# An FFN by seven-product units: 350 tokens become 700 and 348, summed in three PSUM banks, with partial outputs in DRAM

## The chip, the cores and the metric

The kernel runs on one core of one Trainium2 chip. The metric is the device time of one execution in microseconds (us), and the median of several executions is compared. The engines of the core run side by side, each with its own queue of instructions: TensorE (PE for matmuls, PEld for weight loads), VectorE (DVE), ScalarE (ACT), GpSimd (POOL) and SyncE (SP), which here only issues DMAs.

## The reference

One inference step of a two-layer trunk: an SSD (Mamba-2) mixer, a feed-forward network (FFN), an RG-LRU mixer, and a second FFN, with RMS norms before and after each. 1048 tokens go through it: 8 sample tokens, 16 meta tokens and 1024 prompt tokens. The change is in the FFN alone, which runs twice, once in each layer:

```python
D_MODEL = 1024
D_FF = 4 * D_MODEL

def sq_relu_mlp(x, w1, w2):
    h = jax.nn.relu(x @ w1)
    return (h * h) @ w2

# in the trunk, for layer i
h = rms_norm(x, p["norm_ffn_pre"][i])
x = x + rms_norm(sq_relu_mlp(h, p["ffn_w1"][i], p["ffn_w2"][i]), p["norm_ffn_post"][i])
```

All inputs and outputs are float32.

## The kernel before

**Numbers.** Features lie on the 128 partitions and tokens along the rows. Every float32 matrix is split into two float16 parts, hi and lo, and a product of two 128-row tiles takes three matmuls (hi by hi, hi by lo, lo by hi) that add up in PSUM. The tokens are cut into chunks of 350, 350 and 348 (`CW`, `WC`).

**Weights.** They come from DRAM in strips of 1 MB (1024 rows by 256 columns) on SP's queue, into a buffer `ws` of which there are two. A lane of work (`wlane`, `wconv`) turns strip after strip into float16 parts: DVE finds a bound, POOL spreads it over the partitions (`wgb`), a few DVE instructions of one column make the scale, ACT writes hi and DVE lo (`split`) into a buffer `wh`, of which there are five. `self.ahead` limits how many buffers may be ready ahead of their use; a strip of the kinds `H` and `S` (below) takes two, `wh` and `wp`.

**Order of work.** The code writes the matrix products in order and calls `tick()` between them; a tick lets every other lane (weights, norms, sums) emit one step. The engine queues are filled from this by a planner that knows instruction costs, but each engine then works strictly through its own queue.

**The FFN.** The hidden units are taken in four blocks `b` of 1024. For each block the first product gives the hidden units (four strips of `w1`), which are squared and stored as parts in `H`; the second product (four strips of `w2`) adds its part of the output to `acc`, a float32 buffer in SBUF. In the first product of block 0 (`first_phase`, then strip 3) and in the second product of block 3 (`last_phase`, which also runs the norms) every product is done in full, three matmuls for each tile of the sum (`bundle`). The others use Winograd's form of Strassen's algorithm: a strip gives two tiles of 128 outputs, the contraction is taken as pairs of tiles, the chunk as two halves of tokens, and seven products of quarters (`product`) replace eight. For this the sums of the quarters of the weights (`sums`, made by POOL in the strip's own buffer), of the input (`input_sums`, into `TT`) and of the hidden units (`t_sums`, into `HT`) are needed as float16 parts. `t_sums` is a chain over three engines: four POOL subtractions, then ACT writes hi and DVE lo. In the second product only the first `NSUM = 2` of four pairs go by the seven products; the others are added as plain quadrants (`quadrant`).

**A unit** (`unit`) is one strip by one chunk: seven products with 175 (174) moving columns, in seven half banks of four PSUM banks (`pa` to `pd`); eight banks are handed out in turn (`mm`). One ACT copy and five or six DVE instructions add the products up into `z`, which takes one of four buffers (`RBUF`). For the first product `z` then goes through Relu, the squares and `t_sums`; for the second it is added to `acc`.

Of the kernel before, what the change touches and what calls it, by code (L numbers as in the profile page):

```python
# [10 lines left out]
F32 = mybir.dt.float32  # L11
# [12 lines left out]
KT = 8  # L24
# [12 lines left out]
NSUM = 2  # L37
RBUF = 4
# [39 lines left out]
class Queue:  # L78
    """An engine; while hold is set its instructions are issued in program order, and later ones behind them."""
# [38 lines left out]
class Body:  # L118
# [18 lines left out]
    def tab(self, *args, **kw):  # L137
        """An activation whose function needs a table set: these stay in program order."""
# [13 lines left out]
    # ---------------------------------------------------------------- setup  # L152
    def setup(self):
# [28 lines left out]
        # pre-norm gains and group-norm gains scaled by a power of two so that hi/lo fit float16  # L182
# [13 lines left out]
        # the inputs of the ffn leave room for sums of four  # L196
# [15 lines left out]
        self.mad = [self.dram.tile([P, KT * w], F32, name=f"mad{c}") for c, w in enumerate(WC)]  # L212
        a = self.a
# [22 lines left out]
        self.nhid = 0  # L236
        self.wl = self.wlane()
# [7 lines left out]
    def pow2(self, b, n, pool, tag):  # L245
        """p = the power of two at or below b; s = 2^14 / p."""
# [9 lines left out]
    # -------------------------------------------------------------- weights  # L256
# [14 lines left out]
    def split(self, w, st, s, parts):  # L271
        """w = float16 hi and lo parts of st * s, s [P, parts] by contiguous column ranges."""
# [67 lines left out]
    def quarter(self, s, inv):  # L340
        """Scales that leave room for sums of four."""
# [31 lines left out]
    def product(self, ps, i, w, B, T, npair):  # L373
        """ps = one of the seven products of quarters over the first pairs of k tiles, three passes of the float16
        parts; open for the products of the other pairs where there are any."""
# [5 lines left out]
        if npair < 4:  # L381
            add = {2: (0, 0), 3: (0, 1), 4: (1, 0)}.get(i)
        else:
            add = None
        ops = [(lq(l, k), rq(r, k)) for k in range(npair) for l, r in ((0, 0), (0, 1), (1, 0))]
        if add:
            ops += self.quadrant(w, B, npair, *add)
        self.chain(ps, ops)
# [63 lines left out]
    def bundle(self, ps, w, m, act, c, kts=range(KT), first=True, last=True):  # L452
        """ps += sum over k of w[k, m tile]^T act[k, chunk c], three passes of the float16 parts."""
# [14 lines left out]
    def new_u(self):  # L468
        """Float16 parts of the normed input by chunk and k tile."""
# [28 lines left out]
    def normed(self, x, ss, i, hi, lo, pool):  # L498
        """Steps: the pre-norm i of a chunk (its k tiles in x), as float16 parts in hi and lo [P, KT, n]."""
# [1159 lines left out]
```

## Time and profile before

| | |
|---|---|
| runs | 2831.25, 2833.0, 2836.62 us; median 2833.0 us |
| profiled execution | span 2836.7 us from the first to the last instruction; no time of that execution around its span is given, and the span is 3.7 us over the median of the runs |
| instructions | 56933, of them 23209 matmuls |
| PE, DVE, ACT, POOL busy | 2583.1, 2110.1, 1322.6, 691.4 us |
| granted TensorE clock | 0.968 of full speed in the mean |
| FFN of layer 0 | first product of block 0 from about 1004 us; its second product 1095 to 1212; blocks 1 to 3 up to 1668; last product and norms to about 1757 |
| FFN of layer 1 | 2077 to 2167, 2167 to 2737, 2737 to the end |

A line of the profile's groups names the engine, the operation, what it writes and reads (`z<-z,mm`: into `z` from `z` and the PSUM tile `mm`), the shape, the count, the busy time and the mean of one. Nearly all lines of the code appear as line 89, a helper that records every operation, so that instructions are told apart by their tiles and shapes. A table of stages gives, for a stretch of time, what each engine was busy and how many instructions it ran. A table of waits gives who waited for whom: total us, times, and the longest one.

### The profile page before, as it was taken

What the parts mean: (1) busy time and instruction counts of PE and PEld (TensorE: products, weight loads), DVE (VectorE), ACT (ScalarE), POOL (GpSimd) and SP (SyncE); (2) the same over time, 40 slices, a digit from 0 to 9 for tenths busy, and PEclk for the clock granted to TensorE, in tenths of its full rate; (3) what the DMA queues carried; (4) which work ended last, traced back from release to release, by engine and by line L of the source; (5) the groups of instructions that cost most, each with busy time, mean ns of one, the idle gap of its engine ahead of it and who ended that gap; (6) DMA issues with size and microseconds to landing.
All of it is one profiled execution on the core that took longest, in us unless ns stands there. A gap on an engine that the chain in (4) does not pass through costs nothing. (4 is left out here: it accounts for less than half of the span.)

```text
span 2836.7 us, 56933 instructions
## 1 busy us (share of the span) xinstructions
PE 2583.1 (91%) x23209; PEld 2060.6 (73%) x23209; DVE 2110.1 (74%) x5043; ACT 1322.6 (47%) x2148; POOL 691.4 (24%) x972
## 2 busy tenths in 40 slices
PE   4999999999999999789989999979999779989998
PEld 2666666666666667789989976646667779989976
DVE  4889778977873685568778788787685667878776
ACT  4655455545544354344253344658564335253352
POOL 2222111212212024442232201123014452231301
PEclk9999999999999999889999999989999989999999
DMA  3232233223345320101122123110220101111122
GB/s 123 99 119 90 87 107 115 102 88 108 113 159 187 117 106 31 46 31 46 61 72 79 46 110 113 63 62 33 89 108 31 46 31 46 47 45 53 54 73 95
DMA packets 52758, 229.15 MB, mean 81 GB/s; under 512 B 9056, under 2 KB 18416, under 8 KB 31632
## 3 DMA queue, kind: packets, MB, share of 16 engines
q1 hardware_dynamic: 46112, 190.81, 19.1%
q0 software_dynamic: 6384, 34.71, 3.1%
q8 instruction: 181, 2.97, 0.4%
q14 instruction: 81, 0.66, 0.1%
HBM read 186.28 MB, written 39.22 MB: 79 GB/s over the span
## 5 line engine op out<-in xcount | busy, mean ns | idle before, releaser
L89 PEld LDWEIGHTS <-wh 128*128 128x128 f16 x17040 | 1504.0, 99 | 503.7 <-issue 54.7
L89 PE MATMUL mm<-U,wh 128*128 128x350 f16 (+3 forms) x7056 | 989.4, 297 | 20.7 <-ACT rr L89 13.2
L89 PE MATMUL mm<-H,wh 128*128 128x175 f16 (+5 forms) x5664 | 557.7, 253 | 35.3 <-DVE z L89 30.4
L89 PEld LDWEIGHTS <-wp 128*128 128x128 f16 x3888 | 311.0, 99 | 87.6 <-issue 60.5
L89 POOL TENSOR_TENSOR ws<-ws 128x256 f32<-128x256 f32 (+1 forms) x192 | 205.2, 1069 | 328.6 <-DVE wp L89 214.4
L89 DVE TENSOR_TENSOR z<-z,mm 128x175 f32<-128x175 f32 (+3 forms) x648 | 228.4, 370 | 29.2 <-ACT z L89 22.0
L89 POOL PARTITION_ALL_REDUCE wgb<-rm x100 | 55.5, 555 | 656.6 <-issue 338.4
L89 PE MATMUL mm<-U,wp 128*128 128x175 f16 (+1 forms) x1728 | 154.8, 245 | 55.2 <-DVE z L89 55.1
L89 PE MATMUL mm<-TT,wh 128*128 128x175 f16 (+1 forms) x1728 | 167.0, 248 | 10.2 <-ACT TT L89 9.3
L89 ACT ACTIVATE z<-z,ti 128x700 f32<-128x700 f32 (+1 forms) x72 | 63.0, 875 | 183.5 <-DVE z L89 183.5
L89 DVE SCALAR_TENSOR_TENSOR wh<-ws,sw,wh 128x1024 f16<-128x1024 f32 x94 | 122.0, 1320 | 28.3 <-ACT wh L89 28.3
L89 DVE TENSOR_SCALAR qw<-wgb 128x1 f32<-128x1 f32 x103 | 15.5, 150 | 167.3 <-POOL wgb L89 167.1
L89 DVE SCALAR_TENSOR_TENSOR wh<-ws,s,wh 128x256 f16<-128x256 f32 x256 | 114.7, 490 | 11.1 <-ACT wh L89 11.1
L89 DVE TENSOR_REDUCE rm<-ws 128x1 f32<-128x2048 f32 x40 | 91.3, 2281 | 31.2 <-DMA ws<-w 26.7
L89 PE MATMUL mm<-H,wp 128*128 128x175 f16 (+1 forms) x864 | 90.5, 241 | 25.5 <-DVE z L89 23.1
L89 DVE TENSOR_TENSOR ss<-ss,sqt 128x350 f32<-128x350 f32 (+3 forms) x154 | 75.9, 500 | 41.8 <-ACT sqt L89 41.1
L89 ACT ACTIVATE wh<-ws,s 128x512 f16<-128x512 f32 x128 | 83.0, 710 | 48.0 <-POOL ws L89 23.2
L89 DVE SCALAR_TENSOR_TENSOR conv<-pre,ssmall,conv 128x1072 f32<-128x1072 f32 x78 | 103.8, 1330 | 0.1
L89 ACT ACTIVATE wh<-ws,sw 128x2048 f16<-128x2048 f32 x47 | 93.7, 1993 | 14.5 <-DVE sw L89 11.7
L89 DVE TENSOR_SCALAR L<-L,ncs 128x128 f32<-128x128 f32 (+1 forms) x288 | 90.6, 357 | 13.2 <-DMA L<-csd 13.2
L89 DVE TENSOR_TENSOR H<-z,H 128x175 f16<-128x175 f32 (+5 forms) x120 | 81.2, 694 | 23.6 <-ACT H L89 19.5
L89 ACT ACTIVATE pre<-mm,undo 128x8 f32<-128x8 f32 (+1 forms) x104 | 46.5, 474 | 110.7 <-PE mm L89 110.7
(279 smaller groups left out, 4176.9 us busy)
## 6 DMA issues: line engine op xcount, KB each, us to landing
ws<-w SPq DMA_DIRECT2D x64, 1024.0 KB, 4.9
ws<-w_ssd_in SPq DMA_DIRECT2D x24, 1024.0 KB, 5.4
L<-csd SPq DMA_DIRECT2D x64, 256.0 KB, 3.2
ws<-w_lru_in SPq DMA_DIRECT2D x12, 1024.0 KB, 4.9
xd<-xc POOLq DMA_DIRECT2D x6, 1400.0 KB, 5.5
xc<-xd SPq DMA_DIRECT2D x6, 1400.0 KB, 6.0
h<-ssd_h SPq DMA_DIRECT2D x8, 1024.0 KB, 4.9
bc<-bcd SPq DMA_DIRECT2D x8, 1024.0 KB, 4.8
```

The costliest lines, as they stand in the source:

```text
L89: r = f(*args, **kw)
```

## The change

1. `NSUM` goes from 2 to 4: the second product uses seven products over all four pairs, and the extra quadrants fall away. The weights of the second product get all their sums (`sums` with four pairs) and all hidden units of blocks 0 to 2 go through `t_sums`.
2. A unit is a strip by 700 tokens (chunks 0 and 1 together) or by the 348 of chunk 2 (`UN = (350, 174)`: the halves). Its seven products have 350 or 174 moving columns.
3. A unit takes three banks. Products 1, 6, 7 and 4 add up in one bank `y`, 5 and 3 in a bank `s`, and 2 has its own. Between the products the running sums are read: by ACT where a value starts (`copy`), by DVE where it is added to (`plus`), both with the scale.
4. `unit` is a generator with one step for each product. `run_units` lets the first three steps of the next unit run among the last four of the present one, with a tick after each.
5. `acc` is gone. The second product's `z` goes to DRAM (`accd`) by a DMA from POOL's queue, as a plain write for block 0 and with an addition in DRAM for blocks 1 and 2. `last_phase` loads the sums into the room of its output (`pre`).
6. `z` tiles come from two sets of buffers, three of 1400 columns and two of 696 (`ZBUF`); the input's sums use the same. Of the `wp` buffers every second one is a buffer of its own. `ahead` is 4 in place of 3 while the units run. `t_sums` has one more step between ACT and DVE. The hidden units are taken in the order (strip, tokens): the 700 of strips 0 to 3 end before the 348 of strips 2 and 3.

The diff, without comments:

```diff
-NSUM = 2
-RBUF = 4
+NSUM = 4
+UN = (350, 174)
+ZBUF = (3, 2)
...
+        self.accd = [self.dram.tile([P, KT * 2 * n], F32, name=f"accd{u}") for u, n in enumerate(UN)]
...
-            wp = self.wh.tile([P, 2, KT * cols], F16, tag="wh", name="wp")[:, :, :3 * npair * P]
+            if self.nwp % 2:
+                wp = self.fp.tile([P, 2, 3 * 4 * P], F16, tag="wp", name="wp")[:, :, :3 * npair * P]
+            else:
+                wp = self.wh.tile([P, 2, KT * cols], F16, tag="wh", name="wp")[:, :, :3 * npair * P]
+            self.nwp += 1
...
-    def chain(self, ps, ops):
+    def chain(self, ps, ops, first=True):
         for n, (l, r) in enumerate(ops):
-            self.nc.tensor.matmul(ps, l, r, start=n == 0, stop=n == len(ops) - 1)
+            self.nc.tensor.matmul(ps, l, r, start=first and n == 0, stop=n == len(ops) - 1, skip_group_check=not first)
...
-        acc = fp.tile([P, 3, KT, CW], F32, tag="acc", name="acc")
-        HT = fp.tile([P, 3, NSUM, 3, 2, CW // 2], F16, name="HT")
+        HT = [fp.tile([P, NSUM, 3, 2, n], F16, name=f"HT{u}") for u, n in enumerate(UN)]
+        H = [fp.tile([P, 3, KT, 2, CW], F16, tag="H", name="H")]
...
+        def ztile(u, name):
+            return fp.tile([P, 4 * UN[u]], F32, tag=f"z{u}", name=name, bufs=ZBUF[u])
+
+        def square(u, b, s, z):
...
+            nc.scalar.activation(z, z, AF.Square)
+            if self.summed(b, s):
+                nc.vector.tensor_tensor(Hv[:, 1, 0, 1], h[:, 0, 1], Hv[:, 0, 0, 1], op=OP.subtract)
+                nc.vector.tensor_tensor(Hv[:, 1, 1], h[:, 1], Hv[:, 0, 1], op=OP.subtract)
+                t = self.t_sums(z.rearrange("p (i n) -> p i n", i=4), Hv[:, :, 0, 0], HT[u][:, s])
+                next(t)
+                self.lanes.append(t)
+                self.sumlanes[u].append(t)
...
+        def hidden(b, s, u):
+            def done(z, ps, ti):
+                n = UN[u]
+                nc.scalar.activation(z[:, :3 * n], z[:, :3 * n], AF.Relu)
+                nc.scalar.activation(z[:, 3 * n:], ps, AF.Relu, scale=ti)
+                square(u, b, s, z)
+            return done
+
+        def add(b, s, u):
+            def done(z, ps, inv):
+                n = UN[u]
+                nc.scalar.activation(z[:, 3 * n:], ps, AF.Copy, scale=inv)
+                o = self.accd[u][:, 4 * n * s:4 * n * (s + 1)]
+                if b == 0:
+                    nc.gpsimd.dma_start(o, z)
+                else:
+                    nc.gpsimd.dma_start(o, z, accum_op=OP.add)
+            return done
+
+        def work(tl):
+            for b in range(4):
+                ws = {}
+                if b:
+                    while tl in self.lanes:
+                        self.tick()
+                    H[0] = fp.tile([P, 3, KT, 2, CW], F16, tag="H", name="H")
+                    for s, u in ((0, 0), (0, 1), (1, 0), (1, 1), (2, 0), (3, 0), (2, 1), (3, 1)):
+                        if s not in ws:
+                            ws[s] = self.wneed()
+                        w, _, ti = ws[s]
+                        yield self.unit(w, self.parts(U, TT[u], u), UN[u], 4, ztile(u, "z"), ti, hidden(b, s, u))
+                if b < 3:
+                    for s in range(4):
+                        w, inv, _ = self.wneed()
+                        for u in range(2):
+                            while any(t in self.lanes for t in self.sumlanes[u]):
+                                self.tick()
+                            yield self.unit(w, self.parts(H[0], HT[u], u), UN[u], NSUM, ztile(u, "z"), inv, add(b, s, u))
+                    if b == 2:
+                        self.ahead = 2
...
+        tl = self.input_sums(U, TT, ztile)
+        self.lanes.append(tl)
+        self.ahead = 4
+        self.run_units(work(tl))
...
+        def pre(piece, m):
+            c, lo, hi = piece
+            d = self.accd[c // 2].rearrange("p (k n) -> p k n", k=KT)
+            o = CW * (c % 2) + lo
+            nc.sync.dma_start(m, d[:, :, o:o + hi - lo])
+
+        def evac2(piece, mm, ps, inv, o):
+            nc.vector.scalar_tensor_tensor(o, ps, inv, o, op0=OP.mult, op1=OP.add)
...
             nc.scalar.activation(hi, src, AF.Copy)
+            yield
             nc.vector.tensor_tensor(lo, src, hi, op=OP.subtract)
...
+    def unit(self, w, BT, n, npair, z, sc, done):
+        nc = self.nc
         B, T = BT
...
+        q = lambda i: z[:, i * n:(i + 1) * n]
+        prod = lambda i: self.product(i, w, B, T, npair)
+        copy = lambda o, ps: nc.scalar.activation(o, ps, AF.Copy, scale=sc)
+        plus = lambda o, ps: nc.vector.scalar_tensor_tensor(o, ps, sc, o, op0=OP.mult, op1=OP.add)
+        y = self.mm()[:, :n]
+        self.chain(y, prod(1))
+        copy(q(1), y)
+        yield
+        x = self.mm()[:, :n]
+        self.chain(x, prod(2))
+        plus(q(1), x)
+        yield
+        s = self.mm()[:, :n]
+        self.chain(s, prod(5))
+        copy(q(2), s)
+        yield
+        self.chain(y, prod(6), first=False)
+        copy(q(0), y)
+        yield
+        self.chain(y, prod(7), first=False)
+        plus(q(2), y)
+        yield
...
+        self.chain(s, prod(3), first=False)
+        plus(q(0), s)
+        yield
+        self.chain(y, prod(4), first=False)
+        done(z, y, sc)
+        yield
+
+    def run_units(self, units):
+        cur = None
+        for nxt in units:
+            for g in ((cur, nxt, nxt, cur, nxt, cur, cur) if cur else (nxt, nxt, nxt)):
+                next(g)
+                self.tick()
+            cur = nxt
+        for _ in range(4):
+            next(cur)
+            self.tick()
```

More of the change, by code (lines that the diff above doesn't have):

```diff
@@ L371, in sums, with product @@
         yield
-    def product(self, ps, i, w, B, T, npair):
+    def product(self, i, w, B, T, npair):
         w, wp = w
@@ L380, in product @@
         rq = {1: B(0, 0), 2: B(1, 0), 3: B(1, 1), 4: T(2), 5: B(0, 1), 6: T(0), 7: T(1)}[i]
[L381 to L384, printed above, removed]
         ops = [(lq(l, k), rq(r, k)) for k in range(npair) for l, r in ((0, 0), (0, 1), (1, 0))]
-        if add:
-            ops += self.quadrant(w, B, npair, *add)
-        self.chain(ps, ops)
+        if i in (2, 3, 4):
+            ops += self.quadrant(w, B, npair, *{2: (0, 0), 3: (0, 1), 4: (1, 0)}[i])
+        return ops
     def quadrant(self, w, B, npair, i, l):
@@ L577, in last_phase @@
             if pre is not None:
-                pre(c, m)
+                pre(piece, m)
             part = lambda k, c: tuple(z[:, lo:hi] for z in act(k, c))
@@ L1216, in half_b @@
             ws.append((w, self.undo(inv, self.ginv[:, 4:5])))
-        def pre(c, m):
-            nc.sync.dma_start(m, self.mad[c].rearrange("p (k c) -> p k c", k=KT))
+        def pre(piece, m):
+            nc.sync.dma_start(m, self.mad[piece[0]].rearrange("p (k c) -> p k c", k=KT))
         def evac(piece, mm, ps, inv, o):
@@ new lines, in ffn, with evac @@
+        rs = {}
+        def evac(s, w, m, c, ps):
+            u, n = (1, WC[2]) if c == 2 else (0, 2 * CW)
+            if m == 0 and c != 1:
+                rs[s, u] = ztile(u, "r")
+            o = m * n + (CW if c == 1 else 0)
+            nc.scalar.activation(rs[s, u][:, o:o + WC[c]], ps, AF.Relu, scale=w[2])
+            if m and c:
+                square(u, 0, s, rs.pop((s, u)))
+        def hidden(b, s, u):
[5 more added lines that the diff above has]
+            return done
@@ new lines, in ffn @@
+        self.sumlanes = [], []
+        self.first_phase([self.wneed() for _ in range(3)], act, evac)
+        sp = sctx.enter_context(tc.tile_pool(name=f"sum{l}", bufs=1, side="right", reuse_waits="tile"))
+        TT = [sp.tile([P, 4, 3, 2, n], F16, name=f"TT{u}") for u, n in enumerate(UN)]
+        w = self.wneed()
+        for c in range(3):
+            for m in range(2):
+                ps = self.mm()
+                self.bundle(ps[:, :WC[c]], w[0], m, act, c)
+                evac(3, w, m, c, ps[:, :WC[c]])
+                self.tick()
@@ new lines, in ffn, with pre @@
+        tl = self.input_sums(U, TT, ztile)
+        self.lanes.append(tl)
+        self.ahead = 4
+        self.run_units(work(tl))
+        sctx.close()
+        hact = self.act_of(H[0])
+        self.open_bnd()
+        def pre(piece, m):
+            c, lo, hi = piece
[4 more added lines that the diff above has]
+            nc.vector.scalar_tensor_tensor(o, ps, inv, o, op0=OP.mult, op1=OP.add)
@@ L1317, in ffn, with halves @@
+        ws = [self.wneed()[:2] for _ in range(4)]
+        if l == 0:
+            self.last_phase(ws, hact, 1, self.xd[0], self.xd[1], 2, evac2, pre)
+        else:
+            self.last_phase(ws, hact, 3, self.xd[2], [self.a["y01"][0], self.a["y01"][1], self.a["y2"]], None, evac2, pre)
+            self.drain()
+            self.bndctx.close()
         ctx.close()
+    def halves(self, U, u):
+        if u == 0:
+            return U[:, 0:2]
+        return U[:, 2, :, :, :WC[2]].rearrange("p k s (l n) -> p l k s n", l=2)
@@ L1329, in t_sums, with input_sums @@
             nc.scalar.activation(hi, src, AF.Copy)
+            yield
             nc.vector.tensor_tensor(lo, src, hi, op=OP.subtract)
-    def input_sums(self, U, TT, fp):
+    def input_sums(self, U, TT, ztile):
         nc = self.nc
-        for c in range(3):
-            n = WC[c] // 2
+        for u, n in enumerate(UN):
             for k in range(4):
-                f = fp.tile([P, 2 * CW], F32, tag="r", name="f", bufs=RBUF)[:, :4 * n]
-                u = U[:, c, 2 * k:2 * k + 2, :, :2 * n]
+                f = ztile(u, "f")
+                q = self.halves(U, u)[:, :, 2 * k:2 * k + 2]
+                fv = f.rearrange("p (j l n) -> p j l n", j=2, l=2)
@@ L1340, in input_sums @@
                 for j in range(2):
[L1341 to L1342 removed]
+                    nc.gpsimd.tensor_tensor(fv[:, j], q[:, :, j, 0], q[:, :, j, 1], op=OP.add)
+                yield from self.t_sums(f.rearrange("p (i n) -> p i n", i=4), q[:, 0, 0], TT[u][:, k])
                 yield
[L1345 to L1348 removed]
@@ L1350, in unit, with parts @@
-    def unit(self, w, BT, c, npair, fp):
+    def parts(self, U, TT, u):
+        v = self.halves(U, u)
+        return (lambda j, l: lambda s, k: v[:, 1 - l, 2 * k + j, s], lambda i: lambda s, k: TT[:, k, i, s])
+    def unit(self, w, BT, n, npair, z, sc, done):
         nc = self.nc
-        n = WC[c] // 2
         B, T = BT
-        pa, pb, pc, pd = (self.mm()[:, :2 * n].rearrange("p (l n) -> p l n", l=2) for _ in range(4))
-        at = {1: pa[:, 0], 6: pa[:, 1], 5: pb[:, 0], 7: pb[:, 1], 3: pc[:, 0], 4: pc[:, 1], 2: pd[:, 0]}
-        z = fp.tile([P, 2 * CW], F32, tag="r", name="z", bufs=RBUF)[:, :4 * n]
-        zv = z.rearrange("p (i n) -> p i n", i=4)
-        c12, p1, u2 = (zv[:, i] for i in range(3))
-        xy = zv[:, 0::3]
-        for i in (1, 6, 5, 7, 3, 4, 2):
-            self.product(at[i], i, w, B, T, npair)
-            if i == 6:
-                nc.scalar.activation(p1, pa[:, 0], AF.Copy)
-                nc.vector.tensor_tensor(u2, p1, pa[:, 1], op=OP.add)
-            if i == 7:
-                nc.vector.tensor_tensor(xy, pb, zv[:, 2:3].to_broadcast([P, 2, n]), op=OP.add)
-                nc.vector.tensor_tensor(u2, c12, pb[:, 1], op=OP.add)
-                self.tick()
-            if i == 4:
-                nc.vector.tensor_tensor(xy, xy, pc, op=OP.add)
-        if npair < 4:
-            self.chain(pd[:, 1], self.quadrant(w[0], B, npair, 1, 1))
-        nc.vector.tensor_tensor(p1, p1, pd[:, 0], op=OP.add)
-        if npair < 4:
-            nc.vector.tensor_tensor(u2, u2, pd[:, 1], op=OP.add)
-        return z
@@ new lines, in unit @@
+        self.chain(s, prod(5))
[7 more added lines that the diff above has]
+        yield
+        if npair < 4:
+            x = self.mm()[:, :n]
+            self.chain(x, self.quadrant(w[0], B, npair, 1, 1))
+            plus(q(2), x)
+        self.chain(s, prod(3), first=False)
+        plus(q(0), s)
+        yield
+        self.chain(y, prod(4), first=False)
```

94 lines of the change are left out of this document (14 added, 80 removed).

## The prediction

> **What bounds the kernel now.** I read first the page, then the busy time by stages, then who ended PE's waits.
>
> ```profile
> PE 2583.1 (91%) x23209; PEld 2060.6 (73%) x23209; DVE 2110.1 (74%) x5043; ACT 1322.6 (47%) x2148; POOL 691.4 (24%) x972
> PEclk9999999999999999889999999989999989999999
> ```
>
> PE is the only engine near full. Its clock falls below nine tenths in four of the 40 slices of 71 us, two of them in layer 0's FFN (1135 to 1277 us) and one in layer 1's (2269 to 2340). The stages of the FFN (first row: full products of 350 columns; then, in layer 0, second product of block 0, first and second of 1, first and second of 2, first of 3; last, all of these in layer 0 and in layer 1):
>
> ```profile
> core 0: us, PE busy (x) PEld busy (x) DVE busy (x) ACT busy (x) POOL busy (x), PEclk, DMA share, GB/s
> 1030.00:1094.00 64.00, 64.00 (x433) 41.75 (x431) 38.59 (x81) 34.07 (x64) 23.09 (x34) 1.00 0.11 37
> 1095.00:1212.00 117.00, 93.89 (x1079) 91.41 (x1077) 70.16 (x177) 41.55 (x80) 59.60 (x86) 0.88 0.11 37
> 1212.00:1312.00 100.00, 84.64 (x1009) 82.86 (x1007) 70.70 (x176) 49.38 (x83) 35.71 (x51) 0.91 0.12 43
> 1312.00:1397.00 85.00, 82.64 (x1078) 81.80 (x1078) 68.36 (x180) 24.90 (x50) 17.96 (x19) 1.00 0.15 51
> 1397.00:1493.00 96.00, 82.62 (x1013) 80.67 (x1010) 73.13 (x176) 46.97 (x78) 29.97 (x42) 0.95 0.19 67
> 1493.00:1581.50 88.50, 84.20 (x1084) 81.88 (x1082) 73.75 (x184) 24.75 (x50) 21.67 (x24) 1.00 0.20 73
> 1581.50:1668.00 86.50, 79.78 (x1010) 78.12 (x1007) 68.82 (x167) 42.73 (x63) 14.30 (x14) 0.98 0.19 68
> 1095.00:1668.00 573.00, 507.78 (x6261) 496.73 (x6258) 424.93 (x1055) 230.29 (x404) 179.22 (x233) 0.95 0.16 56
> 2167.00:2737.00 570.00, 503.36 (x6265) 492.97 (x6262) 415.27 (x1049) 227.69 (x400) 178.57 (x233) 0.95 0.14 48
> ```
>
> Two prices come out of it. A matmul of 350 columns takes 64.00 / 433 = 147.8 ns, one of 175 takes 82.64 / 1078 = 76.7 ns in the stage that hardly waits. By the code the units of a layer are 36 of 84 matmuls and 36 of 90, 6264 in all, or 480 us at 76.7 ns. The stages took 573 and 570, so some 93 and 90 us of each layer are not matmul work. Over the stages of layer 0 (1080 or 1008 matmuls each) this excess is 34, 23, 2, 19, 6 and 9 us. What it waits for, over all of layer 0's stages, then in the second product of block 0, the first of block 1 and the second of block 1 alone (total us, times, longest):
>
> ```profile
> PE mm L89 <- DVE z L89: 53.9, 35, 6.2
> PE mm L89 <- ACT TT L89: 4.6, 1, 4.6
> PE mm L89 <- DVE H L89: 2.8, 1, 2.8
> ...
> PE mm L89 <- DVE z L89: 20.2, 9, 5.3
> ...
> PE mm L89 <- DVE z L89: 10.0, 4, 5.8
> ...
> PE mm L89 <- DVE z L89: 1.2, 3, 0.7
> ```
>
> PE waits for a bank that DVE has not emptied. The timeline of DVE shows why, although DVE is only 74% busy:
>
> ```profile
> 1253.08 0.34 DVE L89 TENSOR_TENSOR H<-z,H 128x175 f16<-128x175 f32 x1 [1.73 <-ACT H L89]
> 1255.51 0.71 DVE L89 TENSOR_TENSOR HT<-z,HT 128x525 f16<-128x525 f32 x1 [2.09 <-ACT HT L89]
> ...
> 1257.66 0.33 DVE L89 TENSOR_TENSOR z<-z,mm 128x175 f32<-128x175 f32 x1
> ```
>
> DVE stands in its queue before the last link of the chain POOL, ACT, DVE of the sums, and the emptying of PSUM (the last line) stands behind it. The first three waits make 61 us; nearly all the rest of the 93 is clock: 12% of 117 us, 9% of 100, 5% of 96 and 2% of 86.5 are 30 us.
>
> **The change part by part.** *Matmuls.* Each layer has 24 strips of units, all with 84 matmuls of 350 and 84 of 174 columns: 2016 x (147.8 + 76.7 ns) = 453 us against 480. That is 28 us per layer for certain, and with the excess gone altogether 120 and 117, 237 in both.
>
> *Emptying PSUM.*
>
> ```profile
> L89 DVE TENSOR_TENSOR z<-z,mm 128x175 f32<-128x175 f32 x165 | 52.2, 329 | 1.7 <-ACT z L89 1.1
> L89 DVE TENSOR_TENSOR z<-z,mm 128x350 f32<-128x350 f32 x47 | 24.1, 512 | 1.7
> L89 DVE SCALAR_TENSOR_TENSOR acc<-z,iq,acc x48: 933/946/1578, 1330.2 to 2662.7; 128x700 f32<-128x700 f32 x32, 128x696 f32<-128x696 f32 x16
> L89 DVE SCALAR_TENSOR_TENSOR U<-mm,winv,acc x56: 331/574/583, 1683.7 to 2826.3; 128x350 f32<-128x350 f32 x32, 128x348 f32<-128x348 f32 x8, 128x224 f32<-128x224 f32 x8, 128x124 f32<-128x124 f32 x8
> L89 ACT ACTIVATE z<-mm 128x175 f32<-128x175 f32 x48 | 14.3, 299 | 1.7 <-PE mm L89 1.7
> L89 ACT ACTIVATE z<-mm,undo 128x350 f32<-128x350 f32 x32 | 17.6, 549 | 32.6 <-PE mm L89 32.6
> ```
>
> Gone from DVE per layer: 36 units of 3 x 0.33 + 2 x 0.51 = 2.01 us, 36 of 2.34, and 24 additions to `acc` of 0.95: 179 us. New: three scaled additions per unit, 0.574 at 350 and some 0.39 at 174 (between the 0.331 and 0.574 of 124 and 350 columns): 24 x 3 x 0.96 = 69 us. ACT loses 72 copies of 0.30 (22 us) and gains three copies per first and four per second unit, 0.55 and some 0.40: 12 x 7 x 0.95 = 80 us.
>
> *More sums* (`NSUM`).
>
> ```profile
> L89 DVE TENSOR_TENSOR H<-z,H 128x700 f16<-128x700 f32 x15 | 13.8, 918 | 0.0
> L89 DVE TENSOR_TENSOR HT<-z,HT 128x525 f16<-128x525 f32 x8 | 5.6, 701 | 5.7 <-ACT HT L89 5.7
> L89 DVE SCALAR_TENSOR_TENSOR wp<-ws,s,wp 128x128 f16<-128x128 f32 x60 | 18.7, 349 | 1.5 <-ACT wp L89 1.4
> L89 ACT ACTIVATE wp<-ws,s 128x128 f16<-128x128 f32 x60 | 19.5, 389 | 26.5 <-DVE s L89 20.0 <-issue 6.4
> L89 ACT ACTIVATE wh<-ws,sq 128x2048 f16<-128x2048 f32 x12 | 23.9, 1995 | 26.5 <-POOL ws L89 26.5
> L89 POOL TENSOR_TENSOR ws<-ws 128x512 f32<-128x512 f32 x48 | 64.9, 1352 | 80.2 <-DVE wp L89 43.5 <-issue 34.4
> L89 POOL TENSOR_TENSOR ws<-ws 128x256 f32<-128x256 f32 x40 | 31.6, 790 | 70.3 <-DVE wp L89 53.2 <-DVE z L89 8.1 <-issue 6.7
> L89 POOL TENSOR_TENSOR z<-z 128x175 f32<-128x175 f32 x32 | 17.0, 547 | 27.7 <-DVE wh L89 13.7 <-DVE wp L89 7.0 <-DVE H L89 6.3
> ```
>
> Twelve strips of `w2` per layer get six more pairs of 0.39 (ACT) and 0.35 (DVE), and their POOL sums go from 0.79 to 1.35 four times: 28, 25 and 27 us. Six more strips of hidden units pass `t_sums`: per strip and 350 tokens 0.70 and some 0.4 (175 columns, between the 0.33 and 0.51 above), 20 us of DVE; for ACT's share I take the same. A POOL subtraction of 350 columns lies between 0.79 and 1.35, say 1.0, so such a strip costs POOL 4 x 1.0 + 4 x 0.55 = 6.2 us, 37 more per layer. The input's sums are as many columns as before.
>
> *Outputs to DRAM.*
>
> ```profile
> xd<-xc POOLq DMA_DIRECT2D x6, 1400.0 KB, 5.5
> mad<-ev POOLq DMA_DIRECT2D x16, 175.0 KB, 2.3
> U<-mad SPq DMA_DIRECT2D x1, 1392.0 KB, 13.7
> L89 POOL DMA_DIRECT2D xd<-xc x9: 533/562/902, 965.7 to 2099.0; - x9
> ```
>
> 24 DMAs per layer, 0.56 us of POOL each, 13 us; in POOL's queue the weights' sums, `wgb` and `t_sums` wait behind one whose `z` is not ready. Plain writes of 700 and 348 KB would land in 2.3 to 5.5 us. No row shows an addition in DRAM: it is no faster than that, and I bound it by the slowest row, 13.7; I take 7, twice the plain one. It is hidden by the buffers: a pair of units takes 84 x 224.5 ns = 18.9 us, `z` is in use for about as long, and two buffers for 348 tokens leave 2 x 18.9 - 18.9 = 19 us for landing, three for 700 leave 38. The loads of `pre` (up to 13.7 us, beside `xc`) are covered by eight banks of 24 x 147.8 ns = 3.5 us each; without that cover the first evacuation would cost PE some 10 us per layer.
>
> Per layer all this gives DVE 425 - 179 + 69 + 25 + 20 = 360 us, ACT 230 - 22 + 80 + 28 + 20 = 336, POOL 179 + 27 + 37 + 13 = 256, all well under PE's 453. No engine takes PE's place by its sum; what counts is the order.
>
> *Bank `y`.* New waits: product 7 after ACT's copy of 6, and 4 after DVE has read 7. Two products lie between, 12 x 76.7 x 2 = 1.8 us at the least and 3.5 at the most; before, a bank had a whole unit. What can stand in front is the 1.995 us of a strip's hi on ACT. The bounds are nothing and, for 96 such waits per layer, some 0.5 us each.
>
> *What excess stays*, by stage of a layer. Second products of blocks 1 and 2: 4 us each (2 and 6 before; DVE has less to do, the banks are tighter; bounds 3 and 10). First product of block 3: 7 (9 before, no sums there; 3 and 12). First products of blocks 1 and 2: before, they exceed that of block 3 by 12, which is the chain of the sums. The chain takes POOL twice as long per stage, but ACT and DVE now have a tick between them: I take 6 on top of 7, 13 each (bounds 7, the chain hidden, and 29, the chain's part doubled). Second product of block 0: the input's sums lie in it, POOL is busiest there and gets more; half of 34 plus the start, 18 (4 and 34). Sum 59, layer 453 + 59 = 512. Saved: 573 - 512 and 570 - 512, **119 us**; 2836.7 - 119 = 2718, and by the 3.7 us that the span is over the median, **2714**. The bounds make 27 and 124 per layer, or 2650 and 2844.
>
> [...]
>
> **The rivals.** *Excess unchanged:* the chain of the sums is longer and waits as before, only the matmuls' 28 us are saved: 2833 - 56 = 2777. For it, POOL's chain; against it, the stage of 85 us with DVE at 80% and no waits to speak of.
>
> *No cold clock:* the waits become short pieces between products, the excess falls to about 27 us: 480 per layer, 573 + 570 - 960 = 183 saved, 2650. For it, clock 1.00 wherever the longest wait is 0.7 us, and 0.88 with waits of 5.3. [...]
>
> *Slower, by bank `y`:* 192 waits in both layers. Since all excess gone is 237 us, it decides from 237 / 192 = 1.23 us per wait; at 1.5 us the kernel takes 2833 - 237 + 288 = 2884. For it, ACT's and DVE's queues with their 2 us pieces; against it, the 1.8 to 3.5 us between.
>
> *Slower, by the additions in DRAM:* with landing over 19 us, second products of blocks 1 and 2 wait; at 40 us a pair of strips takes 59 in place of 38, 16 strips x 10.5 = 168 us more than forecast, 2882. Landing of 34 us eats the 119.
>
> **How the numbers follow.** Forecast (2680 to 2750) 0.48, no cold clock or better 0.19, excess unchanged 0.15 (all faster); about equal 0.04; bank `y` 0.09 and additions 0.05. A measurement of this kernel tells about 0.2%, 5.7 us, from no change. Faster 0.82, same 0.04, slower 0.14. The range 2630 to 2810 leaves out little below 2650 and the slower cases above.
>
> **What would show it.** 4032 FFN unit matmuls per layer in place of 6264; PE's waits in each stage near the list above, under 2 us each; clock near 1.00 outside block 0; DVE near 360 and ACT near 336 us per layer; landings of the additions under 19 us. Wrong if PE waits for ACT's `z` dozens of times by more than 1 us, if DMA landings release `z`, or if second products stand behind POOL.

## The result: slower by 6.2%, 3011 us

| | before | after |
|---|---|---|
| median of the runs on one chip | 2833.7 us | 3010.9 us (3002.9 to 3012.7), ratio 1.0622, 95% interval 1.0606 to 1.0638 |
| span of the profiled execution | 2836.7 us | 3007.3 us |
| units of layer 0, of layer 1 | 573, 570 us | 661, 656.5 us |
| granted clock, whole span | 0.968 | 0.941 |

The forecast was 2714 us, in a range of 2630 to 2810. The page of the kernel after, busy times and clock:

```profile
PE 2603.4 (87%) x18745; PEld 1811.2 (60%) x18745; DVE 2056.2 (68%) x4623; ACT 1461.9 (49%) x2428; POOL 853.5 (28%) x1020
PEclk9999999999999988998989899989997999888999
```

4464 matmuls are gone, as foreseen, and PE is busy for longer. The stages of the FFN, in the prediction's order (busy us of PE, PEld, DVE, ACT, POOL, then the granted clock):

```profile
1094.00:1235.00 141.00, 89.66 (x654) 63.27 (x653) 78.45 (x176) 53.30 (x106) 73.34 (x84) 0.82 0.19 65
1235.00:1340.00 105.00, 84.58 (x668) 61.55 (x666) 59.93 (x111) 55.54 (x88) 42.69 (x41) 0.90 0.12 39
1340.00:1438.00 98.00, 84.22 (x674) 59.73 (x672) 63.14 (x156) 39.81 (x92) 35.37 (x38) 0.91 0.32 73
1438.00:1552.00 114.00, 89.10 (x678) 64.19 (x676) 69.78 (x137) 59.51 (x93) 42.70 (x43) 0.88 0.23 67
1552.00:1656.00 104.00, 86.04 (x683) 60.84 (x682) 62.97 (x152) 42.45 (x95) 36.36 (x38) 0.93 0.37 91
1656.00:1755.00 99.00, 85.49 (x686) 62.41 (x686) 60.09 (x128) 52.53 (x78) 19.06 (x19) 0.90 0.25 74
1094.00:1755.00 661.00, 519.09 (x4034) 371.98 (x4033) 394.36 (x859) 303.14 (x550) 249.53 (x261) 0.89 0.24 68
2253.00:2909.50 656.50, 516.12 (x4041) 371.36 (x4040) 387.26 (x849) 298.72 (x545) 255.09 (x261) 0.90 0.23 62
```

A stage's matmuls are 75.4 us at full clock (84 x 224.5 ns for each of four strips), so the excess is 66, 30, 23, 39, 29 and 24 us, 208 us per layer in place of 59. In layer 0, 142 us of it is PE idle (661 - 519), and in 66 us the matmuls themselves last longer (519 - 453), at granted clocks of 0.82 to 0.93. No engine is full: DVE 60%, ACT 46%, POOL 38%. What PE waits for in layer 0's stages, and what ACT waits for there:

```profile
PE mm L90 <- DVE z L90: 32.3, 14, 6.5
PE mm L90 <- ACT z L90: 30.2, 16, 6.6
PE mm L90 <- ACT wh L90: 27.8, 9, 5.5
PE mm L90 <- ACT H L90: 21.8, 4, 15.4
PE mm L90 <- ACT wp L90: 12.3, 7, 4.9
PE mm L90 <- DVE wh L90: 6.0, 9, 0.9
...
ACT wh L90 <- POOL ws L90: 72.1, 18, 6.9
ACT H L90 <- POOL z L90: 23.2, 9, 5.5
ACT U L90 <- POOL f L90: 23.2, 8, 4.6
ACT HT L90 <- POOL z L90: 21.5, 12, 4.0
ACT z L90 <- DMA accd<-z: 10.8, 3, 3.8
```

Before, PE waited almost only for DVE's `z`. Now weights (`wh`, `wp`) and parts of hidden units (`H`) are late too, and ACT, which makes them, waits for POOL. POOL's groups in the page:

```profile
L90 POOL TENSOR_TENSOR ws<-ws 128x512 f32<-128x512 f32 x192 | 268.4, 1399 | 196.3 <-issue 82.9
L90 POOL TENSOR_TENSOR z<-z 128x350 f32<-128x350 f32 (+1 forms) x128 | 106.2, 841 | 146.9 <-issue 56.2
```

One wait of 6.5 us in the timeline (start, duration; in brackets the idle time before the instruction and who ended it):

```profile
1136.24 1.39 POOL L90 TENSOR_TENSOR f<-U 128x700 f32<-128x700 f16 x1
...
1137.59 2.27 POOL L90 TENSOR_TENSOR ws<-ws 128x512 f32<-128x512 f32 x1
1138.66 0.39 DVE L90 SCALAR_TENSOR_TENSOR z<-mm,iq,z 128x174 f32<-128x174 f32 x1
1139.82 0.92 POOL L90 TENSOR_TENSOR f<-f 128x350 f32<-128x350 f32 x1
1140.69 0.78 POOL L90 TENSOR_TENSOR f<-U 128x348 f32<-128x348 f16 x1
1141.44 0.80 POOL L90 TENSOR_TENSOR f<-f 128x350 f32<-128x350 f32 x1
...
1142.27 0.49 ACT L90 ACTIVATE U<-f 128x350 f16<-128x350 f32 x1 [4.58 <-POOL f L90]
1142.80 0.56 DVE L90 TENSOR_TENSOR U<-f,U 128x350 f16<-128x350 f32 x1 [3.75 <-ACT U L90]
...
1143.28 0.57 DVE L90 SCALAR_TENSOR_TENSOR z<-mm,iq,z 128x350 f32<-128x350 f32 x1
1143.90 0.74 PE L90 MATMUL mm<-HT,wp 128*128 128x350 f16 x2 [6.47 <-DVE z L90]
```

POOL works through its queue without a pause, a sum of the weights among those of the input. ACT stands before POOL's result, DVE before ACT's, and DVE's reading of the bank, ready long before, stands behind that. Three engines, each under two thirds busy over the layer, hold the fourth. This is one instance; the experiments show how much of the 177 us hangs on POOL's sums.

### The profile page after: what moved, and what is told of

Its sections match the earlier page's. It is cut to its first block, busy times and chain, and to the rows that moved or that the text cites. A ratio compares the mean times of both kernels' runs of the same rounds, so it can differ in the third digit from the quotient of the medians.

```text
span 3007.3 us, 47744 instructions
## 1 busy us (share of the span) xinstructions
PE 2603.4 (87%) x18745; PEld 1811.2 (60%) x18745; DVE 2056.2 (68%) x4623; ACT 1461.9 (49%) x2428; POOL 853.5 (28%) x1020
## 5 line engine op out<-in xcount | busy, mean ns | idle before, releaser
L90 PEld LDWEIGHTS <-wh 128*128 128x128 f16 x13008 | 1244.3, 100 | 760.5 <-issue 113.4
L90 PE MATMUL mm<-U,wh 128*128 128x350 f16 (+2 forms) x6480 | 992.9, 311 | 72.2 <-ACT wh L90 33.9
L90 PE MATMUL mm<-H,wh 128*128 128x350 f16 (+4 forms) x2496 | 334.0, 289 | 35.9 <-ACT wh L90 14.5
L90 POOL TENSOR_TENSOR ws<-ws 128x512 f32<-128x512 f32 x192 | 268.4, 1399 | 196.3 <-issue 82.9
L90 PE MATMUL mm<-HT,wh 128*128 128x174 f16 (+1 forms) x1152 | 179.8, 304 | 58.8 <-ACT z L90 37.6
L90 PE MATMUL mm<-H,wp 128*128 128x174 f16 (+1 forms) x1152 | 150.5, 282 | 40.0 <-ACT H L90 28.6
L90 PE MATMUL mm<-U,wp 128*128 128x174 f16 (+1 forms) x1152 | 152.0, 289 | 22.0 <-ACT wp L90 21.2
L90 PE MATMUL mm<-TT,wh 128*128 128x174 f16 (+1 forms) x1152 | 156.4, 286 | 3.5 <-ACT z L90 3.2
L90 POOL TENSOR_TENSOR z<-z 128x350 f32<-128x350 f32 (+1 forms) x128 | 106.2, 841 | 146.9 <-issue 56.2
L90 ACT ACTIVATE z<-z 128x1050 f32<-128x1050 f32 (+2 forms) x104 | 107.7, 1037 | 82.3 <-DVE z L90 81.6
```

The source lines that it names most:

```text
L90: r = f(*args, **kw)
```

## The experiments

Times are medians; ratios are to the kernel before on the same chip (2837 to 2842 us in these comparisons). Edits are shown against the kernel after; where an edit is made in both kernels, the text says "after" and "before".

Every edit passes through the planner, which can then fill the queues in another order. The traces show the same order of DVE's, ACT's and POOL's instructions only with the plain writes, in both of their runs. In the others it differs: with the readings from product 2's bank, for instance, from the 2200th of DVE's 4623 instructions on, and in the last run from the 2267th of 5103, so that "order of the work stay" in the expectation of that run does not hold. Three edits that reorder the queues and leave POOL's instructions as they were (readings from product 2's bank, units without overlap, copies by DVE) changed the time by 9, 1 and 1 us. Reordering alone thus was worth little there, but no run separates it from an edit's own effect.

**The parts of the change, one at a time.** First `NSUM` back to 2.

```diff
-NSUM = 4
+NSUM = 2
```

> The changed kernel with NSUM back at 2: units of 700 and 348 tokens, three banks (a fourth for the last quadrant), overlap and DRAM additions stay; half the hidden sums, half the POOL work on the strips of w2. Theory S (the doubled sums: ACT and DVE stand in their queues before POOL, weights and sums come late): PE's waits for ACT's and DVE's wh, wp, H and HT, 77 us in layer 0, should halve and the kernel should fall well below 2920 us although it has 38000 columns (16 us) more per layer. Theory B (bank y and s must be read between two products that add up in them): waits for z, 62 us in layer 0, stay; 2990 to 3040 us. Theory D (the additions in DRAM hold POOL and the z buffers): unchanged but for the columns, 3010 to 3045.

2904.6 us, 1.0242 (1.0222 to 1.0263): 106 us less, although 288 more matmuls (x 112 ns = 32 us) came back. The doubled sums cost 138 us.

Then the readings of bank `y` after products 6 and 7 taken from the bank of product 2 (`x`).

```diff
-        copy(q(0), y)
+        copy(q(0), x)
...
-        plus(q(2), y)
+        plus(q(2), x)
```

> The changed kernel, where the two reads between the products 6, 7 and 4 (ACT's copy to q(0), DVE's addition to q(2)) read the bank of product 2 in place of bank y: same instructions, same sizes, but PE need not wait for them before it adds to y. The sums of a unit are thereby other ones. Theory B: PE's waits for ACT z and DVE z (62 us in layer 0) and the cold clock behind them go, 2870 us or less. Theory S: the queues of ACT and DVE are as before, waits move to the next bank or to the weights: 2970 to 3010. Theory D: 3010.

3002.3 us, 1.0584 (1.0562 to 1.0606): 9 us, the intervals just touch. With POOL's sums as they are, the shared bank costs next to nothing.

Plain writes in place of additions in DRAM.

```diff
-                    nc.gpsimd.dma_start(o, z, accum_op=OP.add)
+                    nc.gpsimd.dma_start(o, z)
```

> The changed kernel, where blocks 1 and 2 write their partial outputs over those of the block before in place of adding to them (the output lacks two of three partial sums): same DMAs and sizes, no addition in DRAM. Theory D: POOL is held 0.5 us less for each of 32 DMAs and they land sooner; if the additions are the cause, below 2900. Theories B and S: POOL's issue 1.04 to 0.55 us is 8 us per layer off the critical engine, and ACT waited for these DMAs 11 us in layer 0: 2995 to 3010.

2983.1 us, 1.0518 (1.0494 to 1.0541): the additions cost 28 us, between the two expectations (below 2900, and 2995 to 3010). Landings are not long: in the median 6.7 us for 700 KB and 4.9 us for 348 KB, against 3.6 and 2.7 when all are plain. The issuing on POOL, all 48 DMAs together (16 of them plain in both), with additions and all plain (ns min/median/max):

```profile
L90 POOL DMA_DIRECT2D accd<-z x48: 542/1037/1495, 1158.6 to 2823.8; - x48
L90 POOL DMA_DIRECT2D accd<-z x48: 542/742/744, 1158.3 to 2800.3; - x48
```

In sum these are 44.9 and 32.1 us of POOL.

Units one after the other, without overlap.

```diff
-            for g in ((cur, nxt, nxt, cur, nxt, cur, cur) if cur else (nxt, nxt, nxt)):
+            for g in ((cur, cur, cur, cur, nxt, nxt, nxt) if cur else (nxt, nxt, nxt)):
```

> The changed kernel with the overlap undone: the four last products of a unit run one after the other, then the first three of the next. Between product 6 and 7 and between 7 and 4 lie then none and one product in place of two. Theory B: every unit waits for ACT's copy and DVE's addition in full, some 1 to 2 us twice for each of 96 units in both layers: 3150 us or more. Theory S: the waits for weights and sums are the same and the bank's add little: 3010 to 3080.

3012.3 us, 1.0624 (1.0603 to 1.0645): the overlap neither costs nor saves anything here.

**Which engine carries it.** The copies out of PSUM by DVE in place of ACT:

```diff
-        copy = lambda o, ps: nc.scalar.activation(o, ps, AF.Copy, scale=sc)
+        copy = lambda o, ps: nc.vector.tensor_scalar(o, ps, sc, None, op0=OP.mult)
```

> The changed kernel with the three copies of a unit out of PSUM on DVE in place of ACT (DVE is 60% busy in the FFN, ACT 46%, but ACT stands before POOL's weight sums for 72 us of layer 0). Theory A (what was new is that ACT empties PSUM, and ACT's queue stands before POOL): PE's waits for ACT z (30 us in layer 0) go, 2950 or less. Theory S (the sums themselves come too late, whoever empties): the waits move to DVE's z and to the weights, within 20 us of 3010.

3009.9 us, 1.0606 (1.0587 to 1.0625): no difference. Which of the two engines makes these copies doesn't matter here.

POOL's sums of `w2` over two pairs of the four, all else as it was:

```diff
         q = lambda i, j, ks=slice(0, npair): v[:, ks, j, P * i:P * i + P]
+        if parts != 1:
+            q = lambda i, j, ks=slice(0, 2): v[:, ks, j, P * i:P * i + P]
```

> The changed kernel, where POOL makes the sums of the w2 strips for two of four pairs only, as before the change (256 columns in place of 512); ACT's and DVE's parts and all matmuls stay, so half of those sums are left out of the product. Theory S-weights (the second product's weights come late because POOL's four sums of a strip grew from 3.2 to 5.4 us): 2950 or less. Theory S-hidden (the doubled sums of the hidden units hold the chain): 2990 to 3010.

2946.1 us, 1.0382 (1.0356 to 1.0408): 65 us, for POOL work of 268 - 220 = 49 us less. The row of POOL's weight sums in its page:

```profile
L90 POOL TENSOR_TENSOR ws<-ws 128x256 f32<-128x256 f32 (+1 forms) x192 | 219.5, 1143 | 221.7 <-issue 111.8
```

And without POOL's subtractions for the hidden units of strips 2 and 3:

```diff
-                t = self.t_sums(..., HT[u][:, s])
+                t = self.t_sums(..., HT[u][:, s], s < 2)
...
-            nc.gpsimd.tensor_tensor(o, o, a, op=op)
+            if sub:
+                nc.gpsimd.tensor_tensor(o, o, a, op=op)
```

> The changed kernel, where POOL's four subtractions are left out for the hidden units of strips 2 and 3 (half of them; their parts are still written by ACT and DVE, without the sums). Theory S-hidden: 2950 or less, as PE's waits for H, HT and z shrink. Theory S-weights: 2990 to 3010.

2942.2 us, 1.0359 (1.0342 to 1.0376): 69 us. Each of the two expectations that blamed one half only (2950 or less for its own half, 2990 to 3010 for the other) is thus half right: both halves of POOL's added work cost about alike. Together they make 134 us, nearly the 138 of the doubled sums. If the two savings add up, which no run tested, ACT's and DVE's share of those sums, which both kernels kept, is hardly seen in that state. Each us of sums taken off POOL gave 1.3 us of time in the first of the two and 0.8 in the second (83 us of subtractions less).

Now the weights' sums moved to DVE, in both kernels (`sums`):

```diff
-        tt = nc.gpsimd.tensor_tensor
+        tt = nc.vector.tensor_tensor
```

> The changed kernel with the four sums of each strip of w1 and w2 on DVE in place of POOL: about 0.6 us each by DVE in place of 1.40, 24 strips a layer, 58 us more on DVE (then some 450 of 660 us) and 134 us less on POOL in both layers. Theory S in the form that POOL is the slow link (ACT's wh waits 72 us in layer 0 for POOL's ws): 2930 or less. If the order of the queues is what counts and not POOL's speed: within 30 us of 3010, with the wait on DVE ws in place of POOL ws.

> The kernel before the change with the sums of the w1 and w2 strips on DVE in place of POOL. Theory L (POOL is the slow link of the chain that brings weights and sums, and the change made that link longer): the kernel before has a shorter link (179 us of POOL per layer against 250) and its PE waited for DVE's z, not for weights, so it gains little: 2790 to 2835. If moving these sums is worth the 200 us that it was worth after the change, whatever the units, then the change itself was not what lengthened the link: 2650 to 2700.

After: 2811.0 us, 0.9896 (0.9878 to 0.9913), 200 us less. Before: 2741.3 us, 0.9653 (0.9627 to 0.9679), 96 us less. The first goes as theory L expected. The second falls between its two expectations: the kernel before, whose PE did not wait for weights, gains far more than theory L said, but half as much as the kernel after. The changed kernel's layers with that edit, and DVE's and POOL's rows in its page:

```profile
1091.00:1651.00 560.00, 485.69 (x4040) 359.43 (x4038) 420.70 (x928) 297.17 (x542) 132.01 (x169) 0.95 0.28 78
2149.00:2711.00 562.00, 482.61 (x4045) 358.13 (x4044) 413.65 (x923) 297.76 (x542) 132.25 (x170) 0.95 0.26 70
```
```profile
L90 POOL TENSOR_TENSOR z<-z 128x350 f32<-128x350 f32 (+1 forms) x128 | 103.9, 825 | 228.5 <-DVE H L90 86.9
L90 DVE TENSOR_TENSOR ws<-ws 128x512 f32<-128x512 f32 x192 | 138.2, 720 | 3.1
```

DVE, the busiest engine but PE, was given 138 us of work in both layers together, and the kernel became 200 us faster: the time was in the chain over POOL, not in any engine's sum. With that edit, first `NSUM` = 2, then the readings from bank `x`:

> The changed kernel with the weights' sums on DVE, and NSUM at 2. With POOL out of the weights' chain the doubled sums should cost little more than their 16 us of columns bring per layer: theory L says within 25 us of 2811, where on POOL the same step was worth 106 us the other way. If the doubled sums hurt for another reason (ACT's and DVE's share): 2760 or less.

> The changed kernel with the weights' sums on DVE, where the two reads between products 6, 7 and 4 read the bank of product 2 in place of bank y (the sums of a unit are thereby other ones). With POOL's link gone the bank could be the next bound: PE still waits 33 us for ACT z and 11 for DVE z in layer 0. Theory B for what is left: 2770 or less. If what stands in ACT's queue is the cause and not the bank: 2795 to 2815.

`NSUM` = 2: 2763.3 us, 0.9735 (0.9709 to 0.9762), still 48 us better, which is outside the 25 us of theory L and 3 us short of its rival. Bank `x`: 2813.6 us, 0.9907 (0.9883 to 0.9932), no difference. The doubled sums still cost some 80 us (48 and the 32 of columns), on POOL in the hidden units' chain or on ACT and DVE. To tell these apart, the hidden units' subtractions went to DVE as well:

```diff
-                t = self.t_sums(..., HT[u][:, s])
+                t = self.t_sums(..., HT[u][:, s], nc.vector)
...
-            nc.gpsimd.tensor_tensor(o, o, a, op=op)
+            (eng or nc.gpsimd).tensor_tensor(o, o, a, op=op)
```

> The changed kernel with the weights' sums on DVE and the four subtractions of the hidden units' sums there too (input's sums stay on POOL): 75 us less on POOL per layer, some 45 more on DVE (then 465 of 560). Theory L: the chain of the hidden sums loses its slow link too (leaving half of it out was worth 69 us on POOL): 2770 or less. If DVE is now full: 2811 or more.

> The kernel before, with the weights' sums and the subtractions of t_sums for hidden units made by DVE instead of POOL (the same edit as in the changed kernel that took 2724 us). Open is whether the change loses by itself once POOL is out of both chains. Theory 'only POOL': with short chains the change earns at least its columns, 28 us a layer, so this kernel takes 2780 us or, if DVE (425 of 573 us busy before) has become the limit here, more. Against it stands already that the weights' sums alone brought the kernel before to 2741. Rival 'the change brings nothing of itself': the kernel before gains from short chains as much or more, 2700 to 2730 us, and the columns are eaten by what else was added (sums of twice as many weights and hidden units, additions in DRAM). Between 2735 and 2760 the change is worth 10 to 35 us of its 56.

After: 2723.9 us, 0.9589 (0.9565 to 0.9612), 87 us less again. Before: 2682.9 us, 0.9443 (0.9416 to 0.9471). "Only POOL" expected 2780 of the second and falls; even the rival's 2700 to 2730 was too high. The kernel before gains as well, and stays ahead by 41 us.

**With POOL out of the chains.** Doubled sums and additions again, on the kernel of 2723.9 us:

> The changed kernel with weights' and hidden sums on DVE and NSUM = 2. Going back to two pairs of sums costs the matmuls about 31 us in both layers by their columns, and takes off DVE six strips' subtractions and parts and two pairs' sums a layer, off ACT their parts. Theory 'the doubled sums cost only through POOL': 2740 to 2755 us, against 2724 with NSUM = 4. Rival 'they cost by any engine': 2680 to 2715, as with the hidden sums on POOL, where NSUM = 2 took 2763 against 2811.

> The changed kernel with weights' and hidden sums on DVE, and plain writes in place of the additions in DRAM (the partial outputs of the last block alone are kept, so the output lacks the others). With the sums on POOL the plain writes saved 28 us. Theory 'the additions cost POOL's time': 32 of them at 1.04 instead of 0.55 us of issuing are 16 us of POOL's queue, ahead of its sums; with few sums left on POOL nothing waits for it, and the time stays at 2724, within 8 us. Rival 'the additions cost landing': z comes free late whoever makes the sums, and 20 to 30 us are saved again, 2695 to 2705.

`NSUM` = 2: 2725.6 us, 0.9592 (0.9562 to 0.9623). Both expectations missed: the doubled sums still cost about what they save in columns, some 32 us, though hardly any of them is on POOL. Plain writes: 2719.2 us, 0.9572 (0.9539 to 0.9605), no clear difference, though the landings again got shorter (6.4 to 4.3 us for 700 KB). The additions' 28 us came with the sums on POOL, as the first theory had it.

The input's sums to DVE too (the same two edits in `input_sums` and `t_sums`), in both kernels:

> The changed kernel with all sums, those of the input too, made by DVE; POOL keeps only wgb and the DMAs. Theory 'POOL in any chain of the sums': the second product of block 0 of each layer loses what it still waits for TT, 5 to 15 us a layer, so 2695 to 2715 us against 2724. Rival 'DVE is now the limit there': the input's sums (some 32 subtractions of 350 columns and as many of 174 a layer, about 0.5 and 0.3 us on DVE) stand ahead of the emptying of PSUM, and the time stays or rises by up to 20 us.

> The kernel before with all sums (weights, hidden units, input) on DVE, the same edit as in the changed kernel that took 2687 us: the pair tells what the change is worth with POOL out of every chain. With weights' and hidden sums on DVE this kernel took 2683; of its 499 and 492 us for the units of a layer 482 and 481 are matmuls, so only some 15 us a layer are left, and 5.4 us of PE's waits are in the second product of block 0. Theory 'the change alone brings nothing': 2660 to 2683 us here, so the changed kernel is equal or up to 27 us slower. Rival 'the change alone is worth its columns': DVE, at 91% already in that stage (81 of 89.5 us), becomes the limit with the input's sums, 2700 us or more.

After: 2686.7 us, 0.9457 (0.9429 to 0.9485), 37 us less where the theory had 29 at the most. Before: 2669.3 us, 0.9413 (0.9387 to 0.9439), as "the change alone brings nothing" expected; this version is faster than the kernel before and the kernel after. Last, the kernel after with all sums on DVE and the readings from bank `x`:

> The changed kernel with all sums on DVE, and the readings after products 6 and 7 taken from the bank of product 2 instead of the shared bank y, so that the products 7 and 4 do not wait for them (the sums of these units are then wrong; amount and order of the work stay). Of its 496 us for layer 0's units 463 are matmuls; PE waits 12.1 us for ACT's z (17 times) and 12.4 us for DVE's z (13 times). Theory 'the shared bank is the next limit once POOL is out': most of these 24 us a layer go, 2640 to 2660 us against 2687. Rival 'the same waits move to other banks' (emptying in order of the queues, three banks a unit): 2677 to 2692.

2654.4 us, 0.9354 (0.9335 to 0.9373): 32 us (29 by the ratios), as the first theory expected. The bank that cost 9 us and then nothing is the likely next limit once POOL is out of the chains: PE's waits for `z` in layer 0 fall from 24.5 us to the one row below; the queues' order changed as well.

```profile
PE mm L90 <- ACT z L90: 6.9, 6, 2.3
```

The layers of the kernel after with all sums on DVE, of the kernel before with all sums on DVE, and of the last run (two rows each):

```profile
1094.30:1590.40 496.10, 463.10 (x4037) 346.91 (x4036) 426.08 (x1010) 286.85 (x523) 27.88 (x47) 1.00 0.31 85
2089.50:2584.60 495.10, 467.66 (x4038) 350.75 (x4037) 417.35 (x1004) 286.61 (x523) 27.66 (x47) 0.99 0.29 77
```
```profile
1092.30:1582.60 490.30, 479.85 (x6266) 477.65 (x6265) 470.48 (x1244) 226.22 (x397) 10.46 (x24) 1.00 0.18 64
2081.20:2565.30 484.10, 478.29 (x6266) 475.85 (x6265) 463.96 (x1245) 226.59 (x396) 10.97 (x24) 1.00 0.16 54
```
```profile
1094.80:1576.40 481.60, 459.09 (x4035) 346.10 (x4034) 424.45 (x1009) 288.12 (x522) 30.84 (x47) 1.00 0.32 89
2075.50:2553.90 478.40, 459.03 (x4034) 347.49 (x4033) 414.70 (x1003) 288.26 (x522) 31.21 (x47) 0.99 0.30 81
```

With all sums on DVE, the change takes 27 us off PE's busy time in both layers (958 - 931, half of the 56 foreseen) and adds 44 us of idle time (33 + 27.4 against 10.5 + 5.8): these two profiled executions are 17 us apart. PE's two largest waits in layer 0, in the first and in the second kernel:

```profile
PE mm L90 <- DVE z L90: 12.4, 13, 2.1
PE mm L90 <- ACT z L90: 12.1, 17, 3.0
```
```profile
PE mm L89 <- DVE z L89: 6.9, 6, 1.7
PE mm L89 <- DVE wh L89: 3.4, 2, 2.0
```

**The sum of it.**

| sums made by DVE | before | after | after over before |
|---|---|---|---|
| none | 2834 us | 3011 us | +177 us |
| weights | 2741 | 2811 | +70 |
| weights, hidden units | 2683 | 2724 | +41 |
| all | 2669 | 2687 | +17 |

160 of the 177 us go when the sums leave POOL: 107 with the weights, 29 with the hidden units, 24 with the input. The order of the steps enters these three; the total does not depend on it. The times of a row come in part from different chips; by the ratios, each to the kernel before on its own chip, the last column is 176, 69, 41 and 12 us. In the last row the intervals of the two ratios overlap slightly, so that what the change costs by itself, 12 or 17 us, is hardly clear of nothing. Which property of POOL costs the 160 us (its time for each sum, the longer DVE instructions beside it, told below, or the step of the chain over to another engine's queue) stays open: moving a sum changes all three.

## Why the prediction was wrong, step by step

- *Matmuls*, 453 us per layer: right. Counts are as foreseen, and with bank and POOL out of the way PE is busy for 459.
- *Engine sums* of 360, 336 and 256 us: DVE 394, ACT 303, POOL 250. Sizes were good but for DVE, where instructions that got longer beside POOL (some 40 us over the medians of their groups in layer 0, 14 before; below) explain most of the 34 us. The sentence drawn from them, "no engine takes PE's place by its sum; what counts is the order", was true, and was then not worked out.
- *What excess stays*, 59 us per layer: this is the step that failed. Measured were 208 and 203 (656.5 - 453). Stage by stage it had 18, 13, 4, 13, 4 and 7 against 66, 30, 23, 39, 29 and 24, all beyond their upper bounds. The upper bound for the chain was the excess before, doubled (7 + 2 x 12 = 31, put at 29). With all bounds the sum reached 2844 us, and the stated range ended at 2810 all the same. But in the kernel before much of the chains lay under matmuls (ACT waited for POOL's `ws` there, and PE never for `wh`), so the excess was only what stood out; a longer chain can come out from under the cover as well. The step had the hidden and input sums alone. That weights might come late had no term at all, since PE never waited for `wh` or `wp` before; it was 46 us of PE's waits in layer 0 (27.8 and 12.3 for ACT's `wh` and `wp`, 6.0 for DVE's `wh`), and moving those sums to DVE gave back the most, 200 us. The row that warned was quoted: ACT's idle time before `wh`, 26.5 us by POOL's `ws`.
- *More sums*: POOL's 27 and 37 us per layer were the right work (250 in all), taken as work beside PE's. In its place the runs showed a price: leaving out the one or the other gave 65 and 69 us.
- *Outputs to DRAM*: landing taken as 7 us, 6.7 and 4.9 measured; right, and "landing" did not decide. What was missed: the issuing was put at 0.56 us, an addition took 1.04, and in the queue that had become the critical one this went with 28 us.
- *Bank `y`*: bounds of nothing and 0.5 us per wait. 9 us for 192 waits is 0.05 us each; with POOL out of the chains 32 us, or 0.17. Both lie inside the bounds and far from the 1.23 that the rival needed.
- *No cold clock* (condition: the waits become short pieces between products): the condition failed, with waits of up to 15.4 us in the second product of block 0 and a granted clock of 0.82 in that stage. Where the longest is 3.0 us the clock is 1.00, in layer 0 of the kernel with all sums on DVE, and the matmuls' 66 us of the 208 shrink to some 10 there (463 - 453). Every stage of layer 0 in the kernel after has a wait of 3.9 us or more and a clock of 0.93 or less; what lowers the clock was not shown.
- *The rivals*: "excess unchanged" named the cause, POOL's chain, but kept its price fixed at 2777 us. Both slower rivals named other mechanisms, and the kernel became slower by neither. Of the signs of being wrong, a second product stood behind POOL, as in the timeline above; ACT's `z` held PE 16 times in layer 0, by 1.9 us in the mean; landings held `z` 3 times there, for 10.8 us of ACT. The forecast took POOL's 24% busy for room.

## What to carry to other kernels

An engine that is 38% busy, as POOL here, can set the time when it is one link of a chain and all links work strictly in order. Price added work there by the wait that the next engine's queue gets, and ask what stands behind that wait. Before more work is put on the slow link, try the same operation on a faster engine: here the kernel before, with its sums on DVE at 96% busy, gained 169 us, more than the 119 forecast for the change. A chain that is hidden now has no measured price; its upper bound is its whole length, not what shows of it today.

## What was not expected of the hardware

**DVE's instructions get longer beside POOL's.** Those that read the strip `ws`, in layer 0 (ns min/median/max), with POOL making the sums and with DVE making all:

```profile
L90 DVE SCALAR_TENSOR_TENSOR wp<-ws,s,wp x120: 336/348/2389, 1108.2 to 1611.9; 128x128 f16<-128x128 f32 x120
L90 DVE SCALAR_TENSOR_TENSOR wh<-ws,s,wh x116: 468/478/3516, 1093.7 to 1754.8; 128x256 f16<-128x256 f32 x116
L90 DVE TENSOR_REDUCE r<-ws x26: 1202/1210/1221, 1102.0 to 1742.8; 128x2 f32<-128x1024 f32 x26
```
```profile
L90 DVE SCALAR_TENSOR_TENSOR wp<-ws,s,wp x108: 342/347/354, 1147.1 to 1480.2; 128x128 f16<-128x128 f32 x108
L90 DVE SCALAR_TENSOR_TENSOR wh<-ws,s,wh x101: 475/480/498, 1100.1 to 1590.0; 128x256 f16<-128x256 f32 x101
```

An instruction of 0.48 us took up to 3.5 us, and the reductions `r`, with one input, at most 1.22. In layer 0 of the kernel after, 31 of the 296 instructions that read `ws` together with `wh` or `wp` took over 1.2 times the median of their group; all 31 ran beside a sum on POOL, as did 9 of the other 265. Of the 26 reductions 7 did, and none was longer. What the instructions take over the median of their group makes some 40 us of DVE and 20 of POOL in layer 0, some 14 and 11 in the kernel before, and under 2 each with all sums on DVE. What makes them longer was not shown. No run tells how much of the 160 us goes through this and how much through POOL's own time, since each move of a sum changes both.

**The same sum is nearly twice as fast on DVE.** 128x512 in float32 took 1267 ns in the median on POOL in the kernel after and 689 on DVE in that with all sums there: 1.84 times.

```profile
L90 POOL TENSOR_TENSOR ws<-ws x192: 1253/1267/2647, 1056.0 to 2878.6; 128x512 f32<-128x512 f32 x192
```
```profile
L90 DVE TENSOR_TENSOR ws<-ws x84: 679/689/694, 1150.9 to 1559.6; 128x512 f32<-128x512 f32 x84
```

**A queue that is 96% busy need not hold PE.** With all sums on DVE the kernel before has DVE busy for 470 of 490 us, and PE stands idle for 10.5 us in that layer.
